# A list scheduler that chooses among orders made with margins, by replays with random lengthening

## The chip, the cores and the metric

The kernel runs on one core of one Trainium2 chip. The metric is the device time of one execution, in microseconds (us). A core has TensorE (PE: matmuls, with weight loads shown apart as PEld), VectorE (DVE), ScalarE (ACT), GpSimd (POOL) and SyncE (SP), which here issues all transfers. Each engine carries out its own list of instructions in order and waits on semaphores for the others.

## The reference

A decoder block on a sequence of 1024 tokens of width 1024, one batch, float32:

```python
cond = silu(c) @ ada_w + ada_b                     # shift, scale, gate, twice
h = modulate(rmsnorm(x, norm1_g), shift1, scale1)
u, v, val, gate = split(h @ w_in + b_in)
y_a = spatial_gating_mixer(gelu(u), gelu(v), ...)  # chunks of 128 tokens
y_b = conformer_conv_mixer(val, gate, ...)         # causal conv, 31 taps, group norm, silu
y = concat(rmsnorm(y_a), rmsnorm(y_b))
x = x + gate1 * (y @ w_out)
h2 = modulate(rmsnorm(x, norm2_g), shift2, scale2)
g_ff, up_ff = split(h2 @ w_ffn_in)                 # d_ff = 2816
x = x + gate2 * ((silu(g_ff) * up_ff) @ w_ffn_out)
return modulate(rmsnorm(x, norm_f_g), shift_f, scale_f)
```

## The kernel before

The tokens are cut into two halves of 512, and the features into tiles of 128 partitions, so that a tile is 128x512. Every matrix product is done with float32 split into two float32r parts, high and low: three matmuls for each product (high by high, low by high, high by low; lines 682 to 684, and line 1073 in the feed-forward part). ScalarE makes the high part, VectorE or GpSimd subtracts it for the low part (lines 665/666, 1065/1066). The feed-forward part uses a seven-product scheme over 2x2 blocks, with banks called A, B and C.

The work comes in these stages. First the conditioning vector and the first norm of half 0; the projections val and gate (`p`) of half 0 while the first weights load. Then the projection u (`pu`), the norm of half 1 (`ssq_n`, `rt_n`), v (`v`), the convolution's taps on VectorE (`cv`, line 1006) with a few on GpSimd (`cp`/`s`, line 1001), the group norm (`gn`), the spatial mixing (`pm`), the second half's `p`, and the output projection (`po`). VectorE also multiplies the conditioning weights (`ada`, line 636) in between. Then the second norm of half 0, and products of the feed-forward part that need half 0 alone, done ahead (`ah`), while half 1 is finished. Then the feed-forward tiles (`B`, `C`, `A` from `w_f`), their products kept in HBM (`acts`), and the down projection in three rounds (`fa` by `w_d`). The last norm (`ssq_nf`, `rt_nf`, lines 1345 to 1377) and the output steps (lines 1399 and 1401) end the program, in three pieces of the tokens.

A norm's sums are made by small matmuls against a column of ones (line 727, 32 columns wide); a root on ScalarE (line 730), a reciprocal on VectorE (line 731), and small matmuls that spread the result (line 737).

The order of the instructions on each engine isn't the order in which the program writes them. At its end `fix_order` takes the instructions, makes a graph of their dependences, tile buffers and PSUM banks, and runs a list scheduler over it. `forward` goes through time: on each of the five engines the instruction that is ready and has the best rank is taken. `backward` does the same from the end and gives each instruction its tail, which is the rank of the next `forward`. Durations come from formulas (`duration`), transfers from a model of one queue, `Clock` holds the engines, the port that VectorE and GpSimd share, and TensorE's throttle, and `Slots` the tile buffers. A first `forward` in program order and three rounds give four orders; the one whose planned end is earliest is taken, and each instruction is tied to the one before it on its engine, without a semaphore. SyncE's list of transfers is ordered in the same way, within written orders such as that of the first loads (`in_turn`).

Of the kernel before, what the change touches and what calls it, by code (L numbers as in the profile page):

```python
# [67 lines left out]
ENGINES = ("PE", "DVE", "Activation", "Pool", "SP")  # L68
SIGNAL = {"PE": 0.043, "DVE": 0.024, "Activation": 0.024, "Pool": 0.068, "SP": 0.05}
TABLES = ("Sqrt", "Silu", "Sigmoid", "Gelu")  # L70
TABLE_LOAD = 1.295
LOAD_WAIT, STORE_WAIT, LOAD_RATE, STORE_RATE = 2.05, 1.29, 350e3, 376e3
LOAD_GAP, STORE_GAP, TURN_GAP = 0.07, 0.24, 0.3
DMA_ISSUE = 0.44
DMA_AHEAD = 0.5
SHORT_ROWS = 1.15
CLOCK_WINDOW = 3.4133


class Step:  # L80
# [373 lines left out]
def backward(g, rank, follows):  # L454

    import heapq
    count = len(g.steps)
    before = [sorted(s.before) for s in g.steps]
    need, at, tail = [len(s.after) for s in g.steps], [0.0] * count, [0.0] * count
    for old, new in follows:  # L460
        for n in g.first[new]:
            for m in g.final[old]:
                if m != n:
                    before[n].append(m)
                    need[m] += 1
    ready, waiting = ({e: [] for e in ENGINES} for _ in range(2))
    clock = Clock()
    for s in g.steps:
        if not need[s.n]:
            heapq.heappush(waiting[s.engine], (0.0, s.n))  # L470
    for _ in range(count):
        t, e = pick(clock, ready, waiting)
        while waiting[e] and waiting[e][0][0] <= t + 1e-6:
            n = heapq.heappop(waiting[e])[1]
            heapq.heappush(ready[e], (rank[n], n))
        s = g.steps[heapq.heappop(ready[e])[1]]
        if s.dma:
            begin = max(t, clock.queue)
            clock.queue = begin + s.bytes / (LOAD_RATE if s.load else STORE_RATE) + LOAD_GAP
            end = clock.queue - LOAD_GAP + (LOAD_WAIT if s.load else STORE_WAIT)  # L480
            clock.free[e] = t + DMA_ISSUE
        else:
            begin, end = clock.run(s, t)
        tail[s.n] = end
        for n in before[s.n]:
            need[n] -= 1
            other = g.steps[n].engine
            if (n, s.n) in g.turns:
                at[n] = max(at[n], begin + DMA_ISSUE)
                if not need[n]:  # L490
                    heapq.heappush(waiting[other], (at[n], n))
                continue
            at[n] = max(at[n], begin + s.issue - (s.finish - s.issue) if other == e == "PE" else end + SIGNAL[other])
            if not need[n]:
                heapq.heappush(waiting[other], (at[n], n))
    return tail


def fix_order(tc, edges, stacked, reusing, rounds=3):

    g = Graph(list(tc.nc.cur_bb.bb.instructions), edges, stacked, reusing)
    order, done, follows = forward(g, list(range(len(g.steps))))
    best = max(done), order
    for _ in range(rounds):
        tail = backward(g, [-t for t in done], follows)
        order, done, follows = forward(g, [-t for t in tail])
        best = min(best, (max(done), order), key=lambda b: b[0])
    for steps in best[1].values():
        for earlier, later in zip(steps, steps[1:]):
            tc.add_manual_dep(later.ins, earlier.ins.name,  # L510
                              mybir.DependencyInfo(mybir.DependencyClass.NoSync, mybir.DependencyReason.DATA),
                              reason="fix_order")
# [3 lines left out]
def block_kernel(ctx: ExitStack, tc: tile.TileContext, xT, c, ada, cols, vbias, bs, wsp,  # L516
                 wv, wu, wk, wvg, wo, wf, wfo, wfl, cst, out):
    nc = tc.nc
    V, A, G, PE = nc.vector, nc.scalar, nc.gpsimd, nc.tensor

    edges = []
# [13 lines left out]
    mid = stage.enter_context(tc.tile_pool(name="mid", bufs=1))  # L535
    front = stage.enter_context(tc.tile_pool(name="front", bufs=1))
# [21 lines left out]
    def tmp(name, dt=F32):  # L558
        return front.tile([P, H], dt, tag="tmp", name=name, bufs=N_TMP)
# [285 lines left out]
    for k in range(KD):  # L845
        n = len(nc.cur_bb.bb.instructions)
# [13 lines left out]
        t = tmp(f"t_h1_0_{k}")  # L860
# [283 lines left out]
    ffn = ctx.enter_context(tc.tile_pool(name="ffn", bufs=1, reuse_waits="tile"))  # L1144
# [44 lines left out]
    for f in range(N_AHEAD, N_AHEAD + N_FILL):  # L1189
        t = ffn.tile([P, 2, H], F32, tag="m3", name=f"ahead_{f}", bufs=4)  # L1190
# [67 lines left out]
    order = tile_order()  # L1258
# [236 lines left out]
    output(1)  # L1495
    output(2)

    fix_order(tc, edges, ("mid", "front"), "ffn", 3)


# [79 lines left out]
```

## Time and profile before

| what | us |
|---|---|
| median of 3 runs | 968.09 |
| lowest, highest | 967.17, 968.70 |
| the profiled execution | 967.97 |
| its span, first to last instruction | 965.9 |
| PE busy in the span | 950.5 |
| DVE busy | 871.7 |
| ACT busy | 474.0 |
| POOL busy | 408.6 |

The transfers moved 184.24 MB, 191 GB/s in the mean. In a row of the timeline the columns are start, duration, engine, line, operation, output and inputs, shapes, count, and in brackets the idle time before it with what ended it. In a row of stretches they are the stretch, its length, then busy time and count of PE, PEld, DVE, ACT and POOL, then the granted TensorE clock, the share of the DMA engines, and GB/s. In a row of groups the first number after the bar is the busy time in all, the second the mean of one in ns, and after the second bar stands the idle time before them. The duration of a matmul in the trace is longer than its distance to the next, since matmuls overlap in the array.

### The profile page before, as it was taken

What the parts mean: (1) busy time and instruction counts of PE and PEld (TensorE: products, weight loads), DVE (VectorE), ACT (ScalarE), POOL (GpSimd) and SP (SyncE); (2) the same over time, 40 slices, a digit from 0 to 9 for tenths busy, and PEclk for the clock granted to TensorE, in tenths of its full rate; (3) what the DMA queues carried; (4) which work ended last, traced back from release to release, by engine and by line L of the source; (5) the groups of instructions that cost most, each with busy time, mean ns of one, the idle gap of its engine ahead of it and who ended that gap; (6) DMA issues with size and microseconds to landing.
All of it is one profiled execution on the core that took longest, in us unless ns stands there. A gap on an engine that the chain in (4) does not pass through costs nothing.

```text
span 965.9 us, 12960 instructions
## 1 busy us (share of the span) xinstructions
PE 950.5 (98%) x4521; PEld 769.6 (80%) x4521; DVE 871.7 (90%) x1236; ACT 474.0 (49%) x756; POOL 408.6 (42%) x241
## 2 busy tenths in 40 slices
PE   8999999999999999999999999999999999999996
PEld 4887777778777778788888888888888888888885
DVE  6999999999999763999999999999879999969956
ACT  5787477643474753564333333333337437227426
POOL 0089988836453413665444444455433100000132
PEclk9999999999999999999999999999999999999998
DMA  9882542343485444844677678867657857415104
GB/s 353 323 310 91 176 152 69 113 174 131 137 282 188 158 136 146 271 173 147 215 245 239 230 237 261 268 211 257 211 177 264 266 172 258 162 33 159 61 1 174
DMA packets 70498, 184.24 MB, mean 191 GB/s; under 512 B 7841, under 2 KB 8353, under 8 KB 70434
## 3 DMA queue, kind: packets, MB, share of 16 engines
q1 hardware_dynamic: 70434, 183.43, 56.5%
q8 instruction: 35, 0.57, 0.2%
q14 instruction: 29, 0.24, 0.1%
HBM read 142.24 MB, written 41.16 MB: 190 GB/s over the span
## 4 chain that ended last, share of the span: by engine, by line
PE 79%; DVE 15%; ACT 2%; DMA 2%; issue 1%; SPq 0%; ACTq 0%; DVEq 0%
PE B L1073 30%; PE C L1073 18%; PE ah L1073 10%; DVE cv L1006 5%; PE A L1073 3%; PE v L682 2%; PE v L684 2%; PE po L682 2%; PE po L684 2%; PE v L683 2%; PE po L683 2%; PE p L684 1%; PE p L683 1%; PE p L682 1%; DVE ada L636 1%
## 5 line engine op out<-in xcount | busy, mean ns | idle before, releaser
L1073 PE MATMUL B<-h,w_f 128*128 128x512 f32 x816 | 189.6, 389 | 0.1
L1073 PEld LDWEIGHTS B<-h,w_f 128*128 128x128 f32 x816 | 153.0, 188 | 32.5 <-ACT x L1291 0.8
L1006 DVE SCALAR_TENSOR_TENSOR cv<-ypad,colt,cv 128x512 f32<-128x512 f32 x216 | 147.0, 744 | 0.2
L1073 PE MATMUL B<-fa,w_d 128*128 128x512 f32 x528 | 124.8, 389 | 0.1
L1073 PE MATMUL C<-h,w_f 128*128 128x512 f32 x528 | 123.4, 389 | 0.0
L1073 PEld LDWEIGHTS B<-fa,w_d 128*128 128x128 f32 x528 | 98.8, 188 | 21.4 <-DVE x L1433 0.7
L1073 PEld LDWEIGHTS C<-h,w_f 128*128 128x128 f32 x528 | 99.1, 188 | 20.6
L1073 PE MATMUL ah<-h,wh_a 128*128 128x512 f32 x320 | 102.4, 396 | 0.3 <-ACT h L699 0.3
L1359 POOL TENSOR_TENSOR sq_nf<-sq_nf,sq_nf 128x512 f32<-128x512 f32 (+1 forms) x15 | 18.0, 1202 | 170.2 <-ACT sq_nf L1353 170.0
L666 POOL TENSOR_TENSOR wl_a<-raw_a,wh_a 128x1024 fp32r<-128x1024 f32 x20 | 49.8, 2488 | 78.2 <-ACT wh_a L665 78.2
L1065 ACT ACTIVATE w_d<-raw_d 128x512 fp32r<-128x512 f32 (+1 forms) x72 | 42.0, 593 | 80.9 <-PE B L1073 32.6
L1065 ACT ACTIVATE w_f<-raw_f 128x512 fp32r<-128x512 f32 x68 | 42.5, 629 | 75.9 <-PE B L1073 41.5
L1316 POOL TENSOR_TENSOR x<-x,up 128x512 f32<-128x512 f32 x20 | 33.2, 1659 | 105.6 <-ACT x L1315 105.6
L1066 DVE TENSOR_TENSOR w_f<-raw_f,w_f 128x512 fp32r<-128x512 f32 x68 | 70.2, 1039 | 2.6 <-ACT w_f L1065 2.5
L1073 PEld LDWEIGHTS ah<-h,wh_a 128*128 128x128 f32 x320 | 60.0, 188 | 15.7 <-ACT h L699 1.4
L1073 PE MATMUL C<-fa,w_d 128*128 128x512 f32 (+1 forms) x291 | 63.9, 370 | 0.0
L1073 PE MATMUL ah<-h,wl_a 128*128 128x512 f32 x160 | 62.5, 390 | 0.0
L1073 PEld LDWEIGHTS C<-fa,w_d 128*128 128x128 f32 x291 | 51.0, 188 | 9.2
L1066 DVE TENSOR_TENSOR fa<-a,fa 128x512 fp32r<-128x512 f32 x77 | 52.4, 720 | 0.4 <-ACT fa L1065 0.4
L1433 DVE SCALAR_TENSOR_TENSOR x<-B,cond,x 128x512 f32<-128x512 f32 x48 | 35.6, 745 | 18.2 <-PE B L1073 18.0
L1066 DVE TENSOR_TENSOR w_d<-raw_d,w_d 128x512 fp32r<-128x512 f32 (+1 forms) x72 | 49.1, 691 | 1.1 <-ACT w_d L1065 1.1
L1065 ACT ACTIVATE fa<-a 128x512 fp32r<-128x512 f32 x77 | 46.1, 625 | 7.1 <-DMA a<-acts 4.0
(265 smaller groups left out, 2111.2 us busy)
## 6 DMA issues: line engine op xcount, KB each, us to landing
acts<-x SPq DMA_DIRECT2D x77, 256.0 KB, 2.9
a<-acts SPq DMA_DIRECT2D x77, 256.0 KB, 4.0
raw_f<-wf SPq DMA_DIRECT2D x32, 512.0 KB, 4.0
ada<-ada SPq DMA_DIRECT2D x24, 512.0 KB, 3.5
x<-ada SPq DMA_DIRECT2D x24, 512.0 KB, 4.4
raw_a<-wf SPq DMA_DIRECT2D x20, 512.0 KB, 3.9
ahead<-ahead SPq DMA_DIRECT2D x40, 256.0 KB, 2.6
ypad<-ada SPq DMA_DIRECT2D x16, 512.0 KB, 5.7
```

The lines of the kernel that those rows point to most:

```text
L636: V.scalar_tensor_tensor(raw, raw, 1.0, cact, op0=ALU.mult, op1=ALU.mult, accum_out=cond[:, j:j + 1])
L666: lo_eng.tensor_tensor(lo[:, cut], raw[:, cut], hi[:, cut].bitcast(F32), op=ALU.subtract)
L682: PE.matmul(acc, shi, mhi, start=start, stop=False)
L683: PE.matmul(acc, slo, mhi, start=False, stop=False)
L684: PE.matmul(acc, shi, mlo, start=False, stop=stop)
L1006: V.scalar_tensor_tensor(accs[j], src, wc, accs[j], op0=ALU.mult, op1=ALU.add)
L1065: A.activation(dst[:, 0, :], src, AF.Copy)
L1066: lo_eng.tensor_tensor(dst[:, 1, :], src, dst[:, 0, :].bitcast(F32), op=ALU.subtract)
L1073: last_mm = PE.matmul(bank[:, cols], s, m[:, cols], start=first and p == 0 and i == 0, stop=p == n - 1 and i == 2, skip_group_check=True)
L1316: G.tensor_tensor(g0, g0, up0, op=ALU.mult)
L1359: G.tensor_tensor(run, run, t, op=ALU.add)
L1433: V.scalar_tensor_tensor(x_tile(k, part), bank[:, cols], ccol(GATE2, k), x_tile(k, part), op0=ALU.mult, op1=ALU.add)
```

## The change

Three constants and three functions are new. `replay` runs given orders through the same clock, buffers and durations as `forward`, but takes on each engine only the next instruction of its list, and returns the planned end. `stretched` makes, for the time of a block, the durations of all engines but TensorE, and the bytes of transfers, larger by a factor of each step. `jittered` replays an order with factors drawn at random: 1 plus the absolute value of a normal draw with a deviation of 0.008 on engines and 0.08 on transfers.

`fix_order` now makes its orders with margins: for each of three pairs (1.01 and 1.05, 1.015 and 1.075, 1.02 and 1.1, for engines and transfers) a first `forward` and four rounds, of which the four rounds' orders are kept: twelve. Each is replayed four times, with the same four seeds for all, on the plain durations with random lengthening. The order with the least sum of the four ends is built.

```diff
+MARGINS = ((1.01, 1.05), (1.015, 1.075), (1.02, 1.1))
+JITTER = (0.008, 0.08)
+TRIALS = 4
...
+@contextmanager
+def stretched(g, factor):
+
+    kept = [(s, s.issue, s.finish, s.port, s.dma and s.bytes) for s in g.steps if s.engine != "PE"]
+    for s, issue, finish, port, size in kept:
+        f = factor(s)
+        if s.dma:
+            s.bytes = size * f
+        else:
+            s.issue, s.finish, s.port = issue * f, finish * f, port * f
+    yield
...
+def jittered(g, order, seed):
+
+    import random
+    rng = random.Random(seed)
+    with stretched(g, lambda s: 1 + abs(rng.gauss(0, JITTER[s.dma]))):
+        return replay(g, order)
+
+
+def fix_order(tc, edges, stacked, reusing, rounds=4):
 
     g = Graph(list(tc.nc.cur_bb.bb.instructions), edges, stacked, reusing)
-    order, done, follows = forward(g, list(range(len(g.steps))))
-    best = max(done), order
-    for _ in range(rounds):
-        tail = backward(g, [-t for t in done], follows)
-        order, done, follows = forward(g, [-t for t in tail])
-        best = min(best, (max(done), order), key=lambda b: b[0])
-    for steps in best[1].values():
+    orders = []
+    for margin in MARGINS:
+        with stretched(g, lambda s: margin[s.dma]):
+            order, done, follows = forward(g, list(range(len(g.steps))))
+            for _ in range(rounds):
+                tail = backward(g, [-t for t in done], follows)
+                order, done, follows = forward(g, [-t for t in tail])
+                orders.append(order)
+    times = [sum(jittered(g, order, seed) for seed in range(TRIALS)) for order in orders]
+    best = orders[times.index(min(times))]
+    for steps in best.values():
...
-    fix_order(tc, edges, ("mid", "front"), "ffn", 3)
+    fix_order(tc, edges, ("mid", "front"), "ffn")
```

More of the change, by code (lines that the diff above doesn't have):

```diff
@@ L496, in backward, with replay @@
     return tail
-def fix_order(tc, edges, stacked, reusing, rounds=3):
-    g = Graph(list(tc.nc.cur_bb.bb.instructions), edges, stacked, reusing)
-    order, done, follows = forward(g, list(range(len(g.steps))))
-    best = max(done), order
-    for _ in range(rounds):
-        tail = backward(g, [-t for t in done], follows)
-        order, done, follows = forward(g, [-t for t in tail])
-        best = min(best, (max(done), order), key=lambda b: b[0])
-    for steps in best[1].values():
+def replay(g, order):
+    place, done, at = dict.fromkeys(ENGINES, 0), {}, [0.0] * len(g.steps)
+    need = [len(s.before) for s in g.steps]
+    slots, clock, table = Slots(g), Clock(True), None
+    for _ in range(len(g.steps)):
+        best = None
+        for e in ENGINES:
+            if place[e] == len(order[e]) or need[order[e][place[e]].n]:
+                continue
+            s = order[e][place[e]]
+            tag, t = slots.blocked_on(s)
+            t = max(t, at[s.n], clock.free[e])
+            if tag is None and (best is None or t < best[0]):
+                best = t, s
+        t, s = best
+        slots.take(s)
+        if s.table not in (None, table):
+            table, t = s.table, t + TABLE_LOAD
+        begin, end = clock.run(s, t)
+        done[s.n] = end
+        if slots.release(s, end + SIGNAL[s.engine]):
+            slots.hand_over()
+        for n in s.after:
+            need[n] -= 1
+            if (s.n, n) in g.turns:
+                at[n] = max(at[n], t + DMA_ISSUE)
+            elif g.steps[n].engine == s.engine and not s.dma:
+                at[n] = max(at[n], clock.free["PE"] if s.engine == "PE" else end)
+            else:
+                at[n] = max(at[n], end + SIGNAL[s.engine])
+        place[s.engine] += 1
+    return max(done.values())
@@ new lines, in stretched @@
+@contextmanager
[5 more added lines that the diff above has]
+            s.bytes = size * f
+        else:
+            s.issue, s.finish, s.port = issue * f, finish * f, port * f
+    yield
+    for s, s.issue, s.finish, s.port, size in kept:
+        if s.dma:
+            s.bytes = size
+def jittered(g, order, seed):
[3 more added lines that the diff above has]
+        return replay(g, order)
```

## The prediction

> **What bounds the kernel now.** I read the page's first two parts, then the chain, then the busy time by stretches, then TensorE's own waits, and last the places where TensorE stands still.
>
> The page's head, its busy shares, and the slices of PE and DVE:
>
> ```profile
> span 965.9 us, 12960 instructions
> ...
> PE 950.5 (98%) x4521; PEld 769.6 (80%) x4521; DVE 871.7 (90%) x1236; ACT 474.0 (49%) x756; POOL 408.6 (42%) x241
> ...
> PE   8999999999999999999999999999999999999996
> ...
> DVE  6999999999999763999999999999879999969956
> ...
> PE 79%; DVE 15%; ACT 2%; DMA 2%; issue 1%; SPq 0%; ACTq 0%; DVEq 0%
> ```
>
> TensorE is busy in all slices but the first and the last, VectorE in most. The last line is the chain that ended last: TensorE carries four fifths of it, VectorE most of the rest. So there are two engines that can set the pace, and the stretch tells which. Busy time by stretches, in the order PE, PEld, DVE, ACT, POOL:
>
> ```profile
> 0.00:16.22 16.22, 11.59 (x87) 5.49 (x87) 8.70 (x22) 9.31 (x18) 0.49 (x8) 1.00 0.88 341
> 16.22:265.00 248.78, 247.67 (x1306) 197.63 (x1307) 246.76 (x358) 153.06 (x225) 161.87 (x87) 1.00 0.51 174
> 265.00:444.40 179.40, 178.53 (x833) 141.41 (x831) 146.00 (x193) 100.82 (x153) 80.04 (x42) 1.00 0.55 188
> 444.40:942.10 497.70, 497.56 (x2193) 411.06 (x2193) 454.13 (x632) 194.14 (x328) 159.40 (x97) 1.00 0.60 196
> 942.10:965.90 23.80, 15.15 (x108) 14.00 (x107) 16.06 (x35) 16.64 (x36) 6.83 (x7) 0.81 0.47 176
> ```
>
> Here is the whole room of any new order. TensorE's idle time is 248.78 - 247.67 = 1.11 us up to 265, 179.40 - 178.53 = 0.87 us up to 444.4, and 497.70 - 497.56 = 0.14 us in the dense feed-forward half: 2.12 us in 926. The granted clock is 1.00 in all three. Up to 265 us VectorE has 248.78 - 246.76 = 2.02 us free too, so there both engines are full. What TensorE waited for between 16.22 and 942.1:
>
> ```profile
> PE p L682 <- ACT h L863: 1.5, 1, 1.5
> PE ssq_n L737 <- DVE rt_n L731: 1.0, 1, 1.0
> PE ah L1073 <- ACT h L699: 0.3, 1, 0.3
> ...
> PE ssq_n L733 <- DVE late L620: 0.2, 1, 0.2
> ```
>
> The first ends with the head, where the first projection begins. No wait there is on a transfer: the transfers are covered, and margins on them buy nothing directly.
>
> **The change part by part.** No instruction is added to the program or removed from it; the replays run when the program is made. Four things change in how the order is found. (1) The orders are made with durations of the engines other than TensorE longer by 1, 1.5 or 2% and transfers by 5, 7.5 or 10%. (2) There are twelve candidates (three margins, four rounds each), none of them made on the plain durations, where there were four (a first pass and three rounds). (3) The choice is by the sum of four replays with random lengthening, not by the planned end. (4) The neighbours on each engine are tied as before. So all costs are costs of order: stalls of TensorE, breaks in its stream, and the tail.
>
> *Stalls.* The largest is in these TensorE rows; below them stand VectorE's rows before it, the mean of its product form elsewhere, and GpSimd's row beside it:
>
> ```profile
> 76.26 0.39 PE L682 MATMUL pu<-h,wh_u 128*128 128x512 f32 x1
> 77.61 1.16 PE L737 MATMUL ssq_n<-rt_n,sel_tok 128*128 128x128 f32 x8 [0.96 <-DVE rt_n L731]
> 78.52 0.48 PE L683 MATMUL pu<-h,wl_u 128*128 128x512 f32 x1
> 78.83 0.40 PE L684 MATMUL pu<-h,wh_u 128*128 128x512 f32 x1
> ```
>
> ```profile
> 66.28 2.12 DVE L636 SCALAR_TENSOR_TENSOR ada<-ada,cact 128x1024 f32<-128x1024 f32 x1
> ...
> 72.29 1.76 DVE L636 SCALAR_TENSOR_TENSOR ada<-ada,cact 128x1024 f32<-128x1024 f32 x1
> ```
>
> ```profile
> L636 DVE SCALAR_TENSOR_TENSOR x<-x,cact 128x1024 f32<-128x1024 f32 x24 | 29.8, 1240 | 0.0
> ```
>
> ```profile
> 71.69 8.23 POOL L1001 TENSOR_TENSOR s<-s,cp 128x512 f32<-128x512 f32 x5
> ```
>
> TensorE stood 0.96 us before the small matmuls that spread the norm, although matmuls of the same projection (pu) came right behind them and went through unhindered. The order was written for a reciprocal that would be ready; VectorE was late. Two of its products took 2.12 and 1.76 us where the same form takes 1.24 in the mean: 0.88 + 0.52 = 1.40 us, more than the whole stall; GpSimd was adding beside the second of them. This is what a margin cures: with 1 to 2% on the some 60 us that VectorE has worked since 16 us, the order expects the reciprocal 0.6 to 1.2 us later and puts three to five pu matmuls first (a plain one takes 0.227, as the dense half's 497.56 / 2193 shows; the one after the break takes 0.31, from 78.52 to 78.83). I take the stall as gone with its refill, 0.31 - 0.23 = 0.08 us: -1.04. The bounds are 0 (it stays) and -1.04. What is late next there: the spread norm feeds the modulated half, with a whole projection of TensorE work in front of it.
>
> The rest of the idle time is 2.12 - 0.96 = 1.16 us, in stalls of 0.3 us and less. Such small ones I count as half cured, -0.58, between 0 and -1.16, since a margin moves each wait and makes others.
>
> *Breaks.* Small matmuls (32 wide) put between full ones break the stream. Two rows' distances give the price, eight in a run and thirty-two in a run:
>
> ```profile
> 196.88 0.39 PE L683 MATMUL p<-h,wl_vg 128*128 128x512 f32 x1
> 197.20 0.42 PE L727 MATMUL ssq_b<-sq_b,ones 128*32 128x128 f32 x8
> 197.55 0.50 PE L684 MATMUL p<-h,wh_vg 128*128 128x512 f32 x1
> 197.89 0.39 PE L682 MATMUL p<-h,wh_vg 128*128 128x512 f32 x1
> ```
>
> ```profile
> 71.62 0.39 PE L682 MATMUL pu<-h,wh_u 128*128 128x512 f32 x1
> 71.94 1.08 PE L727 MATMUL ssq_n<-sq_n,ones 128*32 128x128 f32 x32
> 72.95 0.50 PE L683 MATMUL pu<-h,wl_u 128*128 128x512 f32 x1
> 73.29 0.40 PE L684 MATMUL pu<-h,wh_u 128*128 128x512 f32 x1
> ```
>
> From 196.88 to 197.89 are 1.01 us with two full matmuls (0.45), so eight small ones cost 0.56 us. From 71.62 to 73.29 are 1.67 us, also with two, so thirty-two cost 1.22. Four runs of eight would cost 2.24: each further cut costs (2.24 - 1.22) / 3 = 0.34 us. A new order will cut some runs and join others; nothing in the trace says which way. I take 0, and three cuts either way, 1.0 us, for the range.
>
> *Tail.* The last norm, TensorE and ScalarE:
>
> ```profile
> 954.89 1.16 PE L1345 MATMUL ssq_nf<-ones,sq_nf 128*128 128x1 f32 x8
> ...
> 957.54 1.23 PE L1377 MATMUL ssq_nf<-eye,rt_nf 128*128 128x128 f32 x4 [1.49 <-DVE rt_nf L1375]
> ```
>
> ```profile
> 955.49 1.31 ACT L1401 ACTIVATE of<-of,cond 128x256 f32<-128x256 f32 x3
> 956.70 0.24 ACT L1374 ACTIVATE rt_nf<-ssq_nf,epst 128x2 f32<-128x2 f32 x1
> ```
>
> The sums end at 954.89 + 1.16 = 956.05, the root starts at 956.70, since ScalarE is in three output steps of the quarter before. An order that lets the root go first gains up to 0.65 us; one that puts a further step of 1.31 / 3 = 0.44 us ahead loses that. I take half of the gain, -0.3. The head up to 16.22 us is the first loads and the first norm, whose loads are tied in a written order: 0.
>
> *Sum:* -1.04 - 0.58 + 0 - 0.3 = -1.92: with the profiled execution's 967.97 us (2.07 around its span) that is 966.05; it lies 0.12 us under the median of the runs shown, 968.09, which is nothing here. I say 966.0. The best case is -1.04 - 1.16 - 1.0 - 0.65 = -3.85, so 964.1.
>
> *A rule against this reading.* The trace's PE row shows 98%, and the loads of weights 80%. The Trainium skill, "Perfetto Trace Analysis", section "Identifying the Most-Contended Engine", says that the matmul row is no good measure of headroom and the weight loads' busy share is. By the rows above, the dense half has 411.06 / 497.70 = 82.6% there, the two stretches before it 197.63 / 248.78 = 79.4% and 141.41 / 179.40 = 78.8%; at 82.6% these would be 9.5 and 8.2 us shorter, 17.7 us where my stalls give 2.12. The trace agrees that the room is more than the idle time, but the two fences on breaks show where it lies: in small matmuls, which every order must issue.
>
> **The rivals.** *No change that can be told* (within 0.2%, 1.9 us, about what a measurement of this kernel can tell from no change). The program's matmuls take the same time in every order, and in the dense half, 52% of the span, there are 0.14 us to win. If small stalls come back elsewhere and the tail stays, only the 1.04 us are left, less a cut or two: 967 to 969, say 968.
>
> *Slower: the second norm's chain comes late at 265 us.* In the TensorE rows there,
>
> ```profile
> 265.58 0.39 PE L684 MATMUL p<-h,wh_vg 128*128 128x512 f32 x1
> 265.81 0.39 PE L1073 MATMUL ah<-h,wh_a 128*128 128x512 f32 x1
> ...
> 270.94 0.50 PE L1073 MATMUL ah<-h,wh_a 128*128 128x512 f32 x1 [0.30 <-ACT h L699]
> ```
>
> the last projection (p) ends as the first modulated tile (h) of the next stage arrives, and 5 us later TensorE already waits 0.30 us for another. There is no filler left. VectorE has 2.02 us free in all that time, so an order that puts convolution taps or norm work of VectorE behind work that a margin made look urgent, or that meets GpSimd more often, moves this arrival one for one. One more meeting costs 0.52 to 0.88 us by the products above. Two of them are eaten by the gains above; from five or six on (4 us) it decides. With eight, 5.6 us, less the 2 us gained: 971.6, say 972. Against it: the planned durations fit. The replay's price for a tap is 0.756 us, for a split on VectorE 0.692, for a split on GpSimd 2.381, from its formulas; the trace has
>
> ```profile
> L1006 DVE SCALAR_TENSOR_TENSOR cv<-ypad,colt,cv 128x512 f32<-128x512 f32 x216 | 147.0, 744 | 0.2
> L1066 DVE TENSOR_TENSOR fa<-a,fa 128x512 fp32r<-128x512 f32 x77 | 52.4, 720 | 0.4 <-ACT fa L1065 0.4
> L666 POOL TENSOR_TENSOR wl_a<-raw_a,wh_a 128x1024 fp32r<-128x1024 f32 x20 | 49.8, 2488 | 78.2 <-ACT wh_a L665 78.2
> ```
>
> within 2, 4 and 5%, so a choice among twelve by this clock should pick a good one. For it: real lateness comes in lumps of half a microsecond and more, not in draws of 0.8%. The Trainium skill, "SBUF — State Buffer", section "SBUF: two separate sides", says that VectorE with two SBUF inputs and GpSimd exclude each other for a whole instruction; the 2.12 us row agrees, and by this rule the replays' small draws test too little.
>
> *Slower elsewhere*: the twelve orders are all made for durations that do not occur, and none is as tight as the old one; a few stalls like that at 76 us, three more of 0.96, and two cuts make +3.5: 971.5.
>
> *Much faster*, by the weight loads' share: the small matmuls would have to be joined nearly all; 17.7 us, 950. Nothing in the order's rules aims at it.
>
> **How the numbers follow.** Chances: stalls cured 0.42 (966.0, its own range 964.1 to 966.1); no change 0.19 (968); the late chain 0.25 (972); slower elsewhere 0.12 (971.5); much faster 0.02 (950). So faster 0.44, same 0.19, slower 0.37. Likeliest is the first, and it is only just over the bound. For 8 in 10 the range leaves out the much faster case and the slow cases' upper part: from 963.5 (the best case and half a microsecond) to 973.5 (the late chain with two more meetings, 1.5 us).
>
> **What would show it.** Right: TensorE's list of waits has no 1.0 us on the reciprocal of the second half's first norm, and more pu matmuls stand before the small ones; idle time between 16 and 942 us is 1 us or less; the root before the last norm starts within 0.3 us of the sums. The late chain would show as waits of TensorE for h at the start of the ahead quads, or at the first feed-forward tiles. Wrong is the forecast if the head grows: a margin on transfers that reorders the first loads' users, which I put at 0; or if cuts multiply, which shows in the count of small runs.

## The result and the profile after

The changed kernel takes 970.33 us in the median of 10 runs (969.45 to 972.31), the kernel before in the same comparison 967.13 (10 runs, 966.02 to 969.80). The ratio is 1.0031, with a 95% interval of 1.0023 to 1.0039: slower by 3.0 us, 0.3%. The forecast was 966.0, on the other side of the kernel before. The profiled execution of the changed kernel has 969.83 us, 0.5 under its median; that of before stood 0.8 over its own.

The page's head, its busy shares and the chain that ended last, after (lines of the changed file are 66 higher than before's):

```profile
span 968.2 us, 12969 instructions
...
PE 949.4 (98%) x4521; PEld 768.9 (79%) x4521; DVE 867.3 (90%) x1236; ACT 473.5 (49%) x756; POOL 405.9 (42%) x241
...
PE 93%; DVE 2%; POOL 2%; ACT 1%; DMA 1%; issue 1%; SPq 0%; POOLq 0%; ACTq 0%; DVEq 0%
```

The counts of instructions are the same on every engine. VectorE has left the chain (15% before, 2% now), and the time did not fall with it. Where TensorE lost time shows in the busy time by stretches, after (PE, PEld, DVE, ACT, POOL, clock, share of the DMA engines, GB/s):

```profile
16.22:265.00 248.78, 245.65 (x1293) 195.10 (x1294) 236.44 (x353) 151.61 (x222) 161.92 (x87) 1.00 0.50 175
265.00:444.40 179.40, 177.85 (x832) 141.43 (x831) 147.16 (x194) 100.49 (x151) 80.97 (x43) 1.00 0.53 184
444.40:942.10 497.70, 497.68 (x2196) 411.70 (x2195) 458.24 (x636) 195.29 (x330) 153.80 (x96) 1.00 0.58 197
942.10:968.20 26.10, 17.25 (x120) 15.63 (x118) 17.28 (x37) 17.33 (x37) 8.68 (x9) 0.87 0.43 161
```

TensorE's idle time is 248.78 - 245.65 = 3.13 us up to 265 (before 1.11), 1.55 up to 444.4 (0.87) and 0.02 in the dense half (0.14). Together 4.70 where there were 2.12: +2.58; the first 0.60 of it is a first projection that begins that much later. VectorE is busy 236.44 us up to 265, 10.3 less than before; it has 4.1 us more to do in the dense half. TensorE's waits, after, from the whole span:

```profile
PE p L748 <- ACT h L929: 1.7, 1, 1.7
...
PE pu L748 <- ACT h L765: 1.3, 1, 1.3
PE p L750 <- DVE h L934: 1.2, 1, 1.2
...
PE po L748 <- ACT y_b L1030: 0.7, 1, 0.7
PE gn L1108 <- DVE late L686: 0.6, 1, 0.6
...
PE ssq_n L799 <- DVE late L686: 0.2, 1, 0.2
```

The wait of 1.0 us on the reciprocal is gone. Four new ones stand there: 1.3, 1.2, 0.7 and 0.6 us.

The 1.2 lies at 22 us. VectorE's rows there after, and then TensorE's row:

```profile
21.21 1.22 DVE L732 TENSOR_TENSOR wl_k<-raw_k,wh_k 128x1024 fp32r<-128x1024 f32 x1
22.34 1.22 DVE L702 SCALAR_TENSOR_TENSOR ypad<-ypad,cact 128x1024 f32<-128x1024 f32 x1
...
23.48 0.69 DVE L934 TENSOR_TENSOR h<-t_h,h 128x512 fp32r<-128x512 f32 x1
```

```profile
24.23 0.50 PE L750 MATMUL p<-h,wh_k 128*128 128x512 f32 x1 [1.19 <-DVE h L934]
```

and VectorE's before:

```profile
21.86 0.69 DVE L868 TENSOR_TENSOR h<-t_h,h 128x512 fp32r<-128x512 f32 x1
22.47 1.22 DVE L636 SCALAR_TENSOR_TENSOR ypad<-ypad,cact 128x1024 f32<-128x1024 f32 x1
```

The two neighbours have changed places: a product for which ScalarE waits (ypad, for a small step on cond) now goes ahead of the split for which TensorE stands. The 1.3 lies at 87 us; ScalarE's rows after, with TensorE's under them:

```profile
83.71 0.69 ACT L1005 ACTIVATE ya<-pu,colt 128x512 f32<-128x512 f32 x1
84.30 1.33 ACT L1066 ACTIVATE cp<-ypad,colt 128x512 f32<-128x512 f32 x2
85.53 1.32 ACT L764 ACTIVATE t_h<-t_h,cond 128x512 f32<-128x512 f32 x2
86.75 1.14 ACT L765 ACTIVATE h<-t_h 128x512 fp32r<-128x512 f32 x2
```

```profile
87.42 0.50 PE L748 MATMUL pu<-h,wh_u 128*128 128x512 f32 x1 [1.32 <-ACT h L765]
```

Here two copies for GpSimd's taps (cp) stand ahead of the tile that TensorE wants.

By first and last starts of TensorE's groups (after less before, one execution each): the first projection starts 0.60 us later, u's projection 1.26, v's 2.33, the second half's val and gate end 2.93 later, the output projection 3.42, the last feed-forward bank 3.53; the down projection and the tail win some back, and the last norm's matmul starts 2.35 later. The loss is made in the first 390 us. The 0.60 at its start is the order's only in part. In the new order ScalarE has one more small step on cond (0.28 us) between VectorE's gain and the first h, and TensorE waits 1.7 us for that h in all ten traces with the new order's head, 1.5 in the three with the old one. The rest changes from one execution to the next: in nine runs below that have the new order's head the first projection starts between 16.05 and 16.70 us, in the profiled execution of the changed kernel at 16.82, and with the old order's head at 15.83, 16.22 and 16.32.

### The profile page after: what moved, and what is told of

Its sections match the earlier page's. It is cut to its first block, busy times and chain, and to the rows that moved or that the text cites. A ratio compares the mean times of both kernels' runs of the same rounds, so it can differ in the third digit from the quotient of the medians.

```text
span 968.2 us, 12969 instructions
## 1 busy us (share of the span) xinstructions
PE 949.4 (98%) x4521; PEld 768.9 (79%) x4521; DVE 867.3 (90%) x1236; ACT 473.5 (49%) x756; POOL 405.9 (42%) x241
## 4 chain that ended last, share of the span: by engine, by line
PE 93%; DVE 2%; POOL 2%; ACT 1%; DMA 1%; issue 1%; SPq 0%; POOLq 0%; ACTq 0%; DVEq 0%
PE B L1139 32%; PE C L1139 19%; PE ah L1139 11%; PE A L1139 4%; PE po L748 3%; PE po L749 3%; PE po L750 3%; PE p L750 3%; PE p L748 3%; PE p L749 3%; PE v L748 2%; PE v L749 2%; PE v L750 2%; DMA ypad<-ada 1%; PE pm L1013 1%; PE pu L748 1%
## 5 line engine op out<-in xcount | busy, mean ns | idle before, releaser
L1132 DVE TENSOR_TENSOR w_f<-raw_f,w_f 128x512 fp32r<-128x512 f32 x68 | 73.2, 1085 | 1.7 <-ACT w_f L1131 1.7
```

What stands on the lines that cost most here:

```text
L1132: lo_eng.tensor_tensor(dst[:, 1, :], src, dst[:, 0, :].bitcast(F32), op=ALU.subtract)
```

## The experiments

All orders are built from the changed file, with the choice in `fix_order` replaced. A helper `made(g, margin, rounds)` runs the change's own loop for one margin and a number of rounds; `old` is made with margin 1 and two rounds (the kernel before), `new` with 1.01 and 1.05 and three (the changed kernel). `spliced(g, first, then, cut)` takes from one order the steps that the plan starts before `cut`, and the rest from the other. Ratios are to the kernel before on the same chip.

**Which part of the order loses.** `front_old` has the old order up to 360 us, `front_new` the new one, `first95_old` the old one up to 95 us:

```diff
-    best = orders[times.index(min(times))]
+    best = spliced(g, old, new, 360)     # front_old
+    best = spliced(g, new, old, 360)     # front_new
+    best = spliced(g, old, new, 95)      # first95_old
```

> The order of before for all steps that it plans to begin before 360 us, the order of the changed kernel behind that. Theory 1 (the loss is made in the first 360 us, and the changed order wins a little behind them: in the two traces TensorE is 3.42 us behind at the last matmul of the output projection, and 2.35 us at its last matmul): 967.1 - 1.1 = 966.0 us. Rival (the loss is spread over the run, or a property of orders made with margins as such): half of the loss, 968.7 us.

> The other way round: the order of the changed kernel for all steps that it plans to begin before 360 us, the order of before behind. Theory 1: 967.1 + 3.4 = 970.5 us, at least as slow as the changed kernel. Rival (spread): 968.7 us.

> The order of before for the first 95 us, that of the changed kernel behind. Theory 2 (most is lost in the first 95 us: at the start of the v projection the changed kernel is 2.33 us behind by the traces): 970.3 - 2.3 = 968.0 us. Rival (what is lost early is only lent, since VectorE's chain to the second norm sets the pace up to 265 us): 969.5 to 970.5 us.

Measured: front_old 966.57, ratio 0.9987 [0.9978, 0.9996]; front_new 971.92, 1.0046 [1.0033, 1.0060]; first95_old 968.91, 1.0018 [1.0009, 1.0026]. The front is the whole loss and more: the new order behind 360 us is the better one by 1.3 to 1.5 us, and front_old is a little faster than both kernels. Between the first 95 us and the stretch from there to 360 the loss is split, by the medians 1.3 and 3.0 us (1.0031 - 1.0018 and 1.0018 - 0.9987 of 967), by the last norm's last matmul in the traces 2.3 and 1.0, and by the same matmul counted from each trace's own first projection 1.3 and 1.5; that split stays open.

The two runs with the old order in front also show what the stall of the prediction was. TensorE's rows in front_old, at the same place of the same order:

```profile
76.37 0.39 PE L759 MATMUL pu<-h,wh_u 128*128 128x512 f32 x1
76.59 1.14 PE L814 MATMUL ssq_n<-rt_n,sel_tok 128*128 128x128 f32 x8
77.49 0.47 PE L760 MATMUL pu<-h,wl_u 128*128 128x512 f32 x1
```

No wait: the small matmuls follow at the stream's own distance of 0.22 us. In first95_old it is the same but for 0.2 us. VectorE's first product ahead of the reciprocal took 2.12 us in the kernel before's trace, 1.42 in front_old's and 1.82 in first95_old's. The 0.96 us belongs to the one execution that was profiled, not to the order.

**Is the exchange at 22 us the loss?** `swap` is the new order with the two neighbours exchanged back:

```diff
+    dve = best["DVE"]
+    at = next(i for i, s in enumerate(dve) if s.writes[0].name.startswith("h1_0_1_"))
+    dve[at - 1], dve[at] = dve[at], dve[at - 1]
```

> The changed kernel's order with two neighbours on VectorE exchanged at 22 us: the low part of the second modulated tile (h) goes ahead of a product for the conditioning vector. Theory 3 (TensorE's wait of 1.19 us for that h is lost time): 970.3 - 1.2 = 969.1 us. Rival (the wait at 87 us for the second half's h takes it back, because VectorE's chain sets that one): 970.3 us, with the wait at 87 us grown from 1.3 to 2.5 us.

Measured: 970.57, 1.0034 [1.0022, 1.0047]. The wait of 1.2 us is gone from the list and the time is no shorter. In its trace TensorE is 1.4 to 1.6 us ahead of the changed kernel's from 30 to 680 us, of which 0.76 was there when the first projection began (16.05 for 16.81 us); at 681, 695 and 740 us it gives back 1.0. So in this execution the exchange brought some 0.7 us, and none was left at the end. The two pairs of runs below in which it is the only difference come out otherwise.

**Do the replays rank orders as the chip does?** Three orders made otherwise, and one made and chosen with a planner that leaves out TensorE's throttle. The planner's own figures, which are no chip times, stand in the table further down.

```diff
+    best = made(g, (1.0, 1.0), 3)      # plain_r3
+    best = made(g, (1.02, 1.1), 2)     # wide_r2
+    best = made(g, (1.01, 1.0), 3)     # engines_r3
-    ... Slots(g), Clock(True), None
+    ... Slots(g), Clock(), None        # full_clock, orders of margin 1
```

> An order made on the plain durations, third round. On the plain durations its planned end is 7.2 us later than that of before's order, in the mean of the four replays 6.6 us later. Theory 4 (the chip follows the plan on plain durations, with a few us on top that are alike for all orders): 967.1 + 7.2 = 974.3 us. Theory 5 (the chip's lateness is of the kind that the replays draw): 967.1 + 6.6 = 973.7 us, that is 14 us over the changed kernel in the replays, so the replays put the changed kernel first by far: if they are right in kind, the gap to the changed kernel is 14 us; by theory 4 it is 5.5 us.

> An order made with the widest margins (1.02 and 1.1), second round. Planned end on the plain durations 6.3 us later than before's order; mean of the replays 4.1 us earlier than before's order. Theory 4 (plain plan): 973.4 us. Theory 5 (replays): 963.0 us, faster than before.

> An order made with a margin on engines alone (1.01 and 1.0), third round. Planned end on the plain durations 0.4 us later than before's order; replays 1.6 us earlier than before's and 6.4 us later than the changed kernel's. Theory 4: 967.5 us, well under the changed kernel's 970.3. Theory 5: 976.7 us if the changed kernel's 970.3 is taken as the base.

> The scheduler of before (plain durations, a first pass and three rounds, the earliest planned end), but its clock lets TensorE run at full speed from the start, as the granted clock of 1.00 in the first stretch shows, where the plan of before and of the change has half speed for the first matmuls. Theory 6 (the plan believed TensorE slow at 17 to 24 us and so let VectorE serve other work first, which TensorE then waited for): the waits of TensorE for h before 30 us go, 967.1 - 1 = 966 us. Rival (another order from the same greedy search, as good or bad as the next): 967 to 972 us.

Measured: plain_r3 977.31, 1.0102 [1.0086, 1.0117]; wide_r2 972.77, 1.0057 [1.0042, 1.0072]; engines_r3 969.50, 1.0020 [1.0010, 1.0030]; full_clock 974.14, 1.0077 [1.0060, 1.0094]. The chip puts the five orders (these three with old and new) in the order of their plain planned ends; the replays put the old one last but one. Theory 5 falls on these, theory 4 holds, theory 6 falls.

**VectorE's idle time at 60 us.** In the changed kernel VectorE stands 4.5 us at 60 us, since TensorE fills the first pair of banks later. `p_order` gives TensorE's matmuls of the last k there the old sequence, `p_order_swap` adds the exchange.

```diff
+    ends = {s for s in old["PE"] if s.writes[0].name[:3] in ("p0_", "p1_", "p2_", "p3_")
+            and any(o.name.startswith("h1_0_7_") for o in s.reads)}
+    places = [i for i, s in enumerate(best["PE"]) if s in ends]
+    for i, s in zip(places, [s for s in old["PE"] if s in ends]):
+        best["PE"][i] = s
```

> The changed kernel's order, but TensorE goes through the last step (k = 7) of the first projection in the sequence of before's order, so that its first pair of banks is full after six matmuls and not after some sixteen (2.3 us). Theory 7 (VectorE stood idle for 4.5 us at 55 to 60 us for that pair, and this idle time comes back as TensorE's wait of 1.3 us at 87 us): the idle time falls by some 2 us, the wait at 87 us goes, 970.3 - 1.3 = 969.0 us. Rival (the early idle time of VectorE has nothing to do with it): 970.3 us.

> Both repairs: TensorE's sequence at k = 7 and the exchange on VectorE at 22 us. Theory 7: 970.3 - 1.2 - 1.3 = 967.8 us, since VectorE then also has the time that it lacked later on. Rival (the dense half takes early gains back whatever they are): 970.3 us.

Measured: p_order 970.99, 1.0039 [1.0026, 1.0052]; p_order_swap 969.53, 1.0021 [1.0012, 1.0030]. VectorE's idle time became 2.2 and 1.7 us, and the wait at 87 stayed 1.3: theory 7 falls. The two edits together are perhaps a microsecond better than none, with intervals that overlap. These two runs differ by the exchange alone and ran on one chip: the second is 1.5 us faster in the medians, ten of its eleven times lie under the lowest of the five without, and in the traces the lead of 0.6 us that it has at 61 us is 1.25 at the last norm's last matmul. So the exchange that won nothing in swap wins here.

**Who takes the lent room back?** VectorE is busy 458.24 of 497.70 us in the dense half. `short_new` leaves out three quarters of the columns of the last 24 conditioning products there, which takes 24 us from it; `short_swap` adds the exchange.

```diff
+            w = 256 if j >= GATE2 * 8 else D
-            V.scalar_tensor_tensor(raw, raw, 1.0, cact, ...
+            V.scalar_tensor_tensor(raw[:, 0:w], raw[:, 0:w], 1.0, cact[:, 0:w], ...
```

> The changed kernel's order, with three quarters of the columns left out of the last 24 products for the conditioning vector (gate of the feed-forward part, last shift and scale), which VectorE does in the dense half: some 24 x 0.85 = 20 us less for VectorE there, the planned durations and so the order as they were but for a few steps at the end. The output lacks that part of the conditioning. Theory 8 (the dense half, where VectorE is nearly full, takes back what TensorE gains before it): TensorE's idle time there was 0.02 us in the changed kernel, so nothing is to be had: 970.3 us. Rival (VectorE in the dense half sets the changed kernel's time): 967 us or less.

> The same with the exchange at 22 us, which alone gave nothing (970.57 us): its trace is 1.1 to 1.4 us ahead of the changed kernel's up to 680 us and loses that in three places between 680 and 740 us. Theory 8: with VectorE relieved there the gain stays, 1.2 us less than the run without the exchange: 969.1 us. Rival (the exchange gives nothing for another reason): the same as the run without it, 970.3 us.

Measured: short_new 969.54, 1.0023 [1.0013, 1.0032]; short_swap 968.67, 1.0010 [1.0001, 1.0020]. With VectorE relieved the exchange is worth 0.9 us, where in swap it was worth nothing. The direction is theory 8's, the size is under its 1.2. But p_order_swap gained 1.5 us by the same exchange with VectorE's load as it was (457.73 us in the same stretch), so this pair doesn't show that VectorE's load takes anything back. The rival's 967 us, by which that load sets the time, is not reached.

**Is the wait at 87 us ScalarE's order?** `act_first` puts the four steps of h ahead of the two copies, `act_swap` adds the exchange at 22 us, `three_mended` also TensorE's sequence of p_order.

```diff
+    act = best["Activation"]
+    at = next(i for i, s in enumerate(act) if s.writes[0].name.startswith("t_h1_1_0_"))
+    act[at - 2:at + 4] = act[at:at + 4] + act[at - 2:at]
```

> The new order, but ScalarE makes the first two quads of h of the second half (two t_h of 1.32 us, two h of 1.14 us as pairs) ahead of the two copies for the convolution (1.33 us the pair) that stood in front of them at 84.30 us. Theory 9 (the wait of 1.32 us on TensorE at 87 us is made by ScalarE's order alone): that wait is gone or under 0.3 us, the first projection of the first half ends about 1.2 us earlier than in the new order, and if nothing takes it back the time is 1.0 to 1.2 us under the new order's 970.3, about 969.2. Rival (the room is lent and taken back later, as with the exchange on VectorE alone): the wait goes and the time stays within 0.5 us of 970.3.

> The same, and h ahead of the product ypad on VectorE at 22 us. Theory 9: both waits go, 1.19 and 1.32 us, TensorE stands about 2.3 us ahead of the new order at the end of the first projection, and the time is 968.0 to 968.6. Rival (lent and taken back): 969.5 to 970.5.

> Both of these, and TensorE's sequence for the last k of the first pair of banks as in the old order, which took VectorE's idle time at 60 us from 4.5 to 2.2 and 1.7 us. If the three places are the loss of the first 95 us, as theory 9 with theory 7 has it, this comes to the new order with the old first 95 us: 968.9 (1.0018 of the kernel before). If VectorE's missing work, which these do not give back, is what is left, it stays at 969.5 (1.0021) or above, where the first and third edit alone stood.

Measured: act_first 974.43, 1.0081 [1.0067, 1.0095]; act_swap 974.44, 1.0077 [1.0063, 1.0090]; three_mended 972.90, 1.0066 [1.0053, 1.0079]. The wait at 87 us is gone, and the kernel is 4 us slower. GpSimd's rows in act_first, then TensorE's:

```profile
77.77 6.02 POOL L1073 TENSOR_TENSOR s<-s,cp 128x512 f32<-128x512 f32 x4
87.00 2.51 POOL L1073 TENSOR_TENSOR s<-s,cp 128x512 f32<-128x512 f32 x2 [3.21 <-ACT cp L1072]
89.47 2.52 POOL L772 TENSOR_TENSOR h<-t_h,h 128x512 fp32r<-128x512 f32 x2
```

```profile
88.16 0.50 PE L754 MATMUL pu<-h,wh_u 128*128 128x512 f32 x1 [1.12 <-ACT ya L1011]
88.50 0.40 PE L755 MATMUL pu<-h,wl_u 128*128 128x512 f32 x1
90.79 0.50 PE L756 MATMUL pu<-h,wh_u 128*128 128x512 f32 x1 [1.90 <-POOL h L772]
91.13 0.39 PE L754 MATMUL pu<-h,wh_u 128*128 128x512 f32 x1
...
91.90 0.63 PE L754 MATMUL pu<-h,wh_u 128*128 128x512 f32 x1
...
94.88 0.51 PE L755 MATMUL pu<-h,wl_u 128*128 128x512 f32 x1
```

GpSimd makes the low part of the same tile, in order behind the sums that need the copies. It now stands 3.21 us for them, and TensorE, which got the high part early, waits 1.90 us for the low one, after 1.12 us for a bank that ScalarE frees behind the copies. Then the matmuls take 0.63 us instead of 0.39. The busy time by stretches of act_first shows why, in the column of the granted clock:

```profile
90.00:92.00 2.00, 1.21 (x5) 0.97 (x6) 1.23 (x2) 1.97 (x4) 2.00 (x3) 0.93 0.00 0
92.00:94.00 2.00, 2.00 (x6) 1.54 (x5) 1.51 (x3) 2.00 (x5) 2.00 (x2) 0.50 0.00 0
94.00:96.00 2.00, 2.00 (x8) 1.61 (x7) 1.49 (x3) 1.97 (x4) 2.00 (x3) 0.72 0.00 0
```

The two waits brought TensorE to half its clock for about 3.4 us. u's projection takes 3.3 us longer than in the changed kernel (from 61.64 to 112.70 where that had 62.01 to 109.73). Of this 1.12 + 1.90 - 1.32 = 1.70 are waits, and the seven distances from 91.90 to 94.88, 0.43 us each instead of 0.23, make 1.4. Theory 9 falls: the copies ahead of h were the cheaper side of the choice, and their cover is GpSimd's chain. With TensorE's sequence of p_order added, three_mended is 1.5 us faster than act_swap: what one edit is worth depends on the others.

**Orders picked beforehand.** The seventeen orders' planned ends in the planner's own figures (us; replays: mean of the four; they are no chip times), beside the ratio measured:

| order | plain | replays | ratio |
|---|---|---|---|
| half_r3 (1.005, 1) | 959.44 | 967.33 | 1.0028 |
| before | 959.92 | 971.07 | 1 |
| front_old | 959.92 | 968.90 | 0.9987 |
| engines_r3 (1.01, 1) | 960.30 | 969.46 | 1.0020 |
| first95_old | 960.71 | 966.61 | 1.0018 |
| transfers2_r3 (1.015, 1.02) | 960.73 | 963.12 | 0.9992 |
| after (1.01, 1.05) | 961.58 | 963.08 | 1.0031 |
| swap, p_order, p_order_swap | 961.58 | 963.08 | 1.0034, 1.0039, 1.0021 |
| front_new | 961.58 | 965.15 | 1.0046 |
| narrow_r5 (1.003, 1) | 962.83 | 974.68 | 1.0072 |
| act_first, act_swap, three_mended | 965.15 | 966.61 | 1.0081, 1.0077, 1.0066 |
| wide_r2 (1.02, 1.1) | 966.27 | 966.94 | 1.0057 |
| plain_r3 (1, 1) | 967.10 | 977.64 | 1.0102 |

half_r3, transfers2_r3 and narrow_r5 were chosen to set the two rankings against each other:

```diff
+    best = made(g, (1.005, 1.0), 3)      # half_r3
+    best = made(g, (1.015, 1.02), 3)     # transfers2_r3
+    best = made(g, (1.003, 1.0), 5)      # narrow_r5
```

> An order made with a margin of half a per cent on the engines other than TensorE, none on transfers, third round: by the planner's own figures it ends at 959.44 on plain durations, the lowest of 200 orders made with many margins, and at 967.33 in the mean of its four replays. Theory 4 (the chip ranks orders as the plain plan does): level with the kernel before or below, which is planned at 959.92: 965.5 to 968.5. Theory 5 (the replays rank them): slower than the changed kernel's order, whose replays end at 963.08: above 971.

> An order made with margins of 1.5% on engines and 2% on transfers, third round: planned at 960.73 on plain durations, 963.12 in the replays, where the changed kernel's stands at 961.58 and 963.08. Theory 4: between the kernel before and the changed one, as the order planned at 960.30 was: 968.5 to 970. Theory 5: the same as the changed kernel, 970.3 or a little over.

> An order made with a margin of 0.3% on engines alone, fifth round: planned at 962.83 on plain durations, 974.68 in the replays, among the worst of all there. Theory 4: a little slower than the changed kernel, 971 to 973. Theory 5: the slowest but one of the orders run whole, 977 or more, near the order of the plain third round (977.64 in the replays, measured at 977.31).

Measured: half_r3 971.03, 1.0028 [1.0007, 1.0049]; transfers2_r3 967.73, 0.9992 [0.9972, 1.0012]; narrow_r5 975.18, 1.0072 [1.0048, 1.0096]. Neither theory foresaw these three. By theory 4 half_r3 is 2.5 us too slow, transfers2_r3 1 us too fast and narrow_r5 2 us too slow; by theory 5 transfers2_r3 is 2.6 too fast and narrow_r5 2 too fast, and half_r3 meets its "above 971" by 0.03 us in the median but by the ratios is not slower than the changed kernel. Over all seventeen the rank correlation with the ratio is 0.88 for the plain ends and 0.12 for the replays; over the eight orders that were made whole, with no edit, 0.76 and 0.45. So the plain plan carries most, and what it misses, up to some 3 us, is as large as the change's own effect.

What it misses can be seen in half_r3. TensorE's wait there, and VectorE's rows ahead of it:

```profile
80.53 1.16 PE L806 MATMUL ssq_n<-rt_n,sel_tok 128*128 128x128 f32 x8 [2.47 <-DVE rt_n L800]
```

```profile
59.47 2.94 DVE L705 SCALAR_TENSOR_TENSOR ada<-ada,cact 128x1024 f32<-128x1024 f32 x1 [3.99 <-DMA ada<-ada]
...
67.60 2.31 DVE L705 SCALAR_TENSOR_TENSOR ada<-ada,cact 128x1024 f32<-128x1024 f32 x1
...
73.80 2.08 DVE L705 SCALAR_TENSOR_TENSOR ada<-ada,cact 128x1024 f32<-128x1024 f32 x1
...
77.79 1.81 DVE L705 SCALAR_TENSOR_TENSOR ada<-ada,cact 128x1024 f32<-128x1024 f32 x1
...
79.54 0.94 DVE L800 RECIPROCAL rt_n<-rt_n 128x128 f32<-128x128 f32 x1
```

GpSimd's rows beside them:

```profile
67.55 3.52 POOL L1070 TENSOR_TENSOR s<-s,cp 128x512 f32<-128x512 f32 x2
...
72.28 2.52 POOL L1070 TENSOR_TENSOR s<-s,cp 128x512 f32<-128x512 f32 x2
74.75 2.08 POOL L844 TENSOR_SCALAR_AFFINE_SELECT wt<-wt 128x1024 f32<-128x1024 f32 x1
77.23 4.73 POOL L1070 TENSOR_TENSOR s<-s,cp 128x512 f32<-128x512 f32 x3 [0.40 <-ACT cp L1069]
```

In the planner's own figures the reciprocal starts at 77.07, here at 79.54: VectorE is 2.5 us late, about the wait of 2.47. The last three products, of 2.31, 2.08 and 1.81 us with GpSimd at work beside each, are not what makes it late: the planner, which has VectorE wait for GpSimd's port there, gives them 5.7 us together, and they take 6.2. The first one is: planned at 58.81 with 1.24 us, it starts at 59.47, when its transfer has landed, behind an instruction of GpSimd that began at 58.93 and ends at 61.33, and takes 2.94. That is a lump of the kind that the prediction named, and it falls on the order that was planned tightest. The changed kernel has such products too, ahead of a reciprocal that TensorE does not wait for:

```profile
68.65 2.70 DVE L702 SCALAR_TENSOR_TENSOR ada<-ada,cact 128x1024 f32<-128x1024 f32 x1
...
75.24 1.96 DVE L702 SCALAR_TENSOR_TENSOR ada<-ada,cact 128x1024 f32<-128x1024 f32 x1
...
77.78 0.94 DVE L797 RECIPROCAL rt_n<-rt_n 128x128 f32<-128x128 f32 x1
```

With each ratio taken of 967.13, the four other orders without margin on transfers (plain_r3, engines_r3, half_r3, narrow_r5) come out 8.8 to 11.3 us over their plain ends, the kernel before 7.2, and the three with such a margin (transfers2_r3, wide_r2, after) 5.6 to 8.5. So margins seem to buy a microsecond or two on the chip, on few orders, and they can cost as much in the planned end. One place of it can be seen: for this reciprocal TensorE waits 1.5, 2.5 and 1.4 us in plain_r3, half_r3 and narrow_r5, made with less than 1% on engines, and not at all in the four orders made with 1% or more (engines_r3, after, transfers2_r3, wide_r2); full_clock, with none, has 0.2, and the old order 0 to 0.96. These are single executions, and that such lumps are what margins buy off was not tried by itself.

## Why the prediction was wrong

*The stall, -1.04.* The wait is gone, as forecast, and that was worth nothing. After:

```profile
78.65 0.39 PE L750 MATMUL pu<-h,wh_u 128*128 128x512 f32 x1
78.88 1.06 PE L803 MATMUL ssq_n<-rt_n,sel_tok 128*128 128x128 f32 x8
```

Of u's matmuls 69 now run ahead of the small ones that spread the norm, where 64 did, but not as the filler that the prediction described. They stand ahead of the norm's sums (56 for 49); between the sums and the small ones there are 13 where there were 15. The reciprocal ends 2.9 us behind the sums, where it took 4.5 in the trace before, and 3.4 and 3.6 in the two runs with the old order in front. Those two runs hardly have that wait, so the term was taken from one execution. That execution's 0.84 us above the median of the runs was the hint; the prediction compared it with the median of three runs, 968.09, and so saw none. Nor were the two products that it called late by 1.40 us unusual: their 1.24 is the mean of products in the dense half, and the twelve on ada, theirs among them, take 1.81 in the mean of the same trace.

*The rest of the idle time, half cured, -0.58.* This is the step that failed. The 1.16 us of small waits became 4.10 behind the first projection's start, +2.94 instead of -0.58, and that start came 0.60 later. The prediction counted what a margin could cure and bounded what it could newly make only by a rival. A list scheduler that is given other durations does not repair an order, it makes another one, and every greedy choice in it can fall the other way, as that of ypad and h at 22 us did.

*Breaks, 0 with 1.0 either way.* Counted in the traces from 16.2 to 942 us, small matmuls (sums, norms and group norm) break the stream 35 times where they did 32: three cuts at 0.34, +1.0 us, the upper end. Idle time and cuts together, 2.58 + 1.0 = 3.6 us, are what the last feed-forward bank shows, 3.53.

*Tail, -0.3.* Not found. The root still stands behind three output steps, after:

```profile
958.20 1.31 ACT L1467 ACTIVATE of<-of,cond 128x256 f32<-128x256 f32 x3
959.41 0.24 ACT L1440 ACTIVATE rt_nf<-ssq_nf,epst 128x2 f32<-128x2 f32 x1
```

```profile
957.73 1.05 PE L1411 MATMUL ssq_nf<-ones,sq_nf 128*128 128x1 f32 x8
```

The sums end at 957.73 + 1.05 = 958.78, and the root starts 0.63 us later, 0.65 before.

*Head, 0.* The warning in the prediction's last part, that the forecast is wrong if the head grows, points to about the right place, but not to the cause it gave: the head's 0.60 us are some 0.2 of ScalarE's order and for the rest this execution's, and the order on VectorE and ScalarE loses its time from 22 us on.

*The rivals.* The late chain at 265 us had the larger chance and is refuted: TensorE has no wait for h there, and VectorE, which was to be the one that is full, stands 10 us more. The other slow one, "slower elsewhere", was it: orders made for durations that do not occur, none as tight as the old one, a few stalls and cuts more. It was priced at three stalls of 0.96 and two cuts, 971.5; the trace has 1.32, 1.19, 0.7 and 0.6 and three cuts, and the time is 970.3. Its chance of 0.12 was too small, for one reason: the planner's formulas fit the rows, and from this the prediction argued that the choice among twelve would be good. The same fit speaks for the plain plan that chose the old order. Of the twelve, the order taken has also the earliest plain end (961.58, the next 961.81 and 962.87, in the planner's own figures), so among these the two choices agree; what was given up is the old order itself, since none of the twelve is made on plain durations. Had it been among them, the replays would still have passed it over: they set it 11.1 us above its plain end and the new one 1.5, where on the chip the one is 7.2 above it and the other 8.5.

*The two rules that it weighed.* That weight loads' share measures the room (the Trainium skill, "Perfetto Trace Analysis", "Identifying the Most-Contended Engine") got no support here: that share is 80% before and 79% after, and what moved the time were waits and cuts. The exclusion of VectorE and GpSimd (the Trainium skill, "SBUF — State Buffer", "SBUF: two separate sides") fits half_r3's products of 1.8 to 2.9 us, each with GpSimd at work beside it. The traces bear it out for this form: in all twenty of this case, a 128x1024 product of VectorE with no GpSimd instruction beside it takes at most 1.25 us, and one with GpSimd beside it 1.21 to 3.43.

What is settled: the loss lies ahead of 360 us, in the order, and no one edit there brought it back. What stays open: how it divides over the steps there, since the same exchange won 1.5, 0.9 and in two cases 0 us by what else was in the order, why the lead of swap was given back at 681 to 740 us, and which property of an order the chip's last 3 us depend on.

## What to carry to other kernels

A stall that is read from one execution is a term of the sum only if a second execution of the same order shows it. Where a scheduler's objective is changed, the price is what the new orders lose on the durations that do occur, and it is spread over several small waits. The list of waits is no price list for mending them: the exchange at 22 us cured a wait of 1.2 us and won between 0 and 1.5, and moving the copies at 84 us cured one of 1.3 and lost 4. An edit is best judged against the same order without it, on the same chip, and in more than one order. A planner's clock that ranks whole orders by steps of 5 us is not for that fit to choose among orders 1 to 2 us apart: the few best have to be timed, as front_old (0.1% faster than the kernel before) and transfers2_r3 (not to be told from it) show.

## What the runs showed of the hardware

Two waits of 1.12 and 1.90 us, with two matmuls between them, halved TensorE's granted clock in all three runs that have them: in act_first to 0.50 for 3.4 us (the stretch from 92 to 94 us shows it, with matmuls of 0.63 us), in act_swap for 6.8 us (from 89.1 to 95.9) and in three_mended for 6.8 as well. A single wait of 1.32 us in the changed kernel leaves it at 1.00, and so does one of 2.47 in half_r3, longer than either of the two. The Trainium skill, "TensorE: Matmul & The Clock Gate", section "What's actually happening", has half rate after an idle window of about 3.4 us; the traces agree with the half rate, which lasts one and two times 3.4 us, and show that the idle time need not be in one piece.

A product of VectorE on 128x1024 took 1.25 us at most where no GpSimd instruction ran beside it, and up to 3.43 where one did (twenty traces).
